# RWKV-7 recurrence on one core: the two heads of a pair on opposite partition halves, their matmuls alternating

## The chip, the cores and the metric

The kernel runs on 1 core of a Trainium2 chip. The metric is the device time of one execution in microseconds (us), taken as the median of several runs; less is better. TensorE (PE) does the matmuls, VectorE (DVE), ScalarE (ACT) and GpSimd (POOL) work on tiles, SyncE (SP) issues most transfers (DMA).

## What is computed

The program is a two-layer decoder trunk over 1024 tokens of 1024 channels. Layer 1 is an RWKV-7 time mix (16 heads of 64 channels) and an MLP, layer 2 is sliding-window attention and an MLP. The change lies in the state recurrence of layer 1, which the reference states as:

```python
def step(S, inp):
    r_t, w_t, k_t, v_t, a_t, b_t = inp
    sa = jnp.einsum('bhvk,bhk->bhv', S, a_t)
    S = S * w_t[:, :, None, :] + sa[..., None] * b_t[:, :, None, :] + v_t[..., None] * k_t[:, :, None, :]
    y = jnp.einsum('bhvk,bhk->bhv', S, r_t)
    return S, y
```

Per head, S is 64 x 64. Both kernels compute it in chunks of 64 tokens: within a chunk the dependence of tokens on each other is the inverse T of a triangular 64 x 64 matrix, so that a chunk takes a handful of 64 x 64 products per head.

## The kernel before

The large products (projections, MLP, output products) are float32 split into two 12-bit parts, three matmuls for each (mm3, L134 to L136), on tiles of 128 x 128 weights and 512 or 256 moving columns. The recurrence uses plain float32 matmuls; each of these stands in the trace as two matmul instructions ("rows" below), each with its own weight load.

The recurrence goes over 16 units: 8 blocks of 128 tokens (2 chunks each) times 2 groups of 8 heads (4 pairs). A unit passes through six steps, which the method recurrence calls in the order c i s p f j for most units: prep (p: the factors of the unit after the next), inner (i: inner products of the next unit's chunks, L638), solve (s: the 32 x 32 diagonal blocks of T by substitution, on GpSimd, in and out of DRAM), join (j: T's off-diagonal blocks, 32 x 32 matmuls L693 and L697), chunks (c: the chunks in turn), finish (f: norm, bonus and gate). In a chunk five batches of 8 matmuls (one per head) follow each other: L723 (the old state's and the values' part of u), L728 (their part of y), L733 (T times it, which gives u), L737 (the new state), L742 (u's part of y).

SV has the state (later u) of a head on partitions 0 to 63 and its values on 64 to 127, for all heads alike. So the matmuls of a batch of L723, L733 or L737 write the same 64 partitions of PSUM for all 8 heads; those of L728 and L742 write y by channels, where the odd head of a pair stands on the upper partitions, and so alternate between the two halves (h % 2).

A scheduler orders each engine's instructions from the code's order, priorities and its own estimate of times; the order is fixed when the program is built. The recurrence is emitted as urgent, which puts its instructions ahead of the large products where both are ready; the projections and, for units 8 to 15, the first MLP fill the rest. SP takes its transfers in this fixed order too, weight loads (L269, five tiles "wr") among those of the recurrence.

Of the kernel before, what the change touches and what calls it, by code (L numbers as in the profile page):

```python
# [50 lines left out]
# what follows what in a step of the recurrence: c chunks, i inner, s solve, p prep, j join, f finish;  # L51
# where the next block waits for its part, where the one after it does, elsewhere
# [22 lines left out]
class Trunk:  # L75
# [51 lines left out]
    def split(self, hi, lo, src, engine=None):  # L127
        """hi + lo = src; src is float32 in SBUF."""
# [10 lines left out]
    def consts(self):  # L139
# [19 lines left out]
        # derived columns: 1 - mu, w0 / 2, a0 / 2, k_a / 2, 1 - k_a / 2  # L159
# [6 lines left out]
        # masks of a chunk: rows s (twice), columns t (r side, a side)  # L166
# [7 lines left out]
        # head indicators  # L174
# [12 lines left out]
        # projection of a head's channels onto those of mean 0  # L187
# [6 lines left out]
        # reset of the running sum at each chunk  # L194
# [3 lines left out]
        # rows of the identity, dealt over partitions (js, block, chunk and head)  # L198
# [19 lines left out]
    def rsqrt(self, dst, src, mul, add):  # L218
        """dst = (src * mul + add) ** -0.5 for a narrow tile."""
# [25 lines left out]
    def turn_split(self, rows, gain):  # L245
        """Normalized rows by channels in two parts."""
# [18 lines left out]
    def weight(self, ap, shape, gain=None):  # L265
        """A weight of 2 KB a partition in two parts; gain: the columns of factors of its rows."""
# [11 lines left out]
    def prod_t(self, W, xs, c0, n=P):  # L278
        """[n outputs from c0 on, tokens] = (x W)^T in PSUM."""
# [7 lines left out]
    def prod_n(self, W, xs, j, n=512, gain=None):  # L287
        """Per token tile [P tokens, n] = columns j*n... of x W in PSUM; W has 128 rows for each of xs."""
# [10 lines left out]
    def mlp(self, layer, xt, rows, dst, G=4, between=None, beside=iter(()), pace=1):  # L299
        """xt: the rows, and what is added to them; rows: normalized; between: what is emitted before the last groups."""  # L300
# [35 lines left out]
    def steps(self, hT, n):  # L336
        """Differences of the tokens before and the tokens; none where there is no room for them."""
# [9 lines left out]
    def shifted(self, hT, i, n):  # L347
        """Per tile of channels, token-shifted input i in two parts."""
# [14 lines left out]
    def thin(self, hT, i, n, W, outs):  # L363
        """Input i times W, by tiles of channels; outs: (PSUM for [outputs, tokens], first column of W)."""
# [10 lines left out]
    def lora_out(self, W2, u, off, dst, pt):  # L375
        """tanh((u W2 + off) / 2) to DRAM, a channel tile at a time; u is float32 [64, tokens]."""
# [23 lines left out]
    def gate_in(self, hT, pt):  # L400
        """The gate's inner products, a channel tile at a time."""
# [18 lines left out]
    def gate_out(self, pt):  # L420
        """The gate to DRAM, a channel tile at a time."""
# [31 lines left out]
    def rows(self, pt):  # L453
        """Per 256 tokens, the normalized rows of a part; the first ones ahead."""
# [8 lines left out]
    def channels(self, pairs, hT):  # L463
        """Per 256 tokens, the normalized input by channels, with the token before; yields per two tiles of channels."""
# [17 lines left out]
    def project(self, pt, hT, left):  # L482
        """The projections of a part; left: what is left to do for the one before. Returns both for the next part."""
# [17 lines left out]
        # where there is room for both inputs, receptance and keys of a group before those of the next  # L501
# [15 lines left out]
        def prod(i, o):  # L517
            """Receptance, keys."""
# [8 lines left out]
        for group in groups:  # L527
# [3 lines left out]
            # and the squared norms of the keys' directions  # L531
# [24 lines left out]
            # 1 / max(|kk|, 1e-12)  # L556
# [6 lines left out]
    def spread(self, src, ps):  # L563
        """[P channels of a head pair, tokens] in PSUM = the values of the pair's heads, src: [P tokens, tiles, 2]."""
# [9 lines left out]
    def prep(self, blk, g):  # L574
        """Factors of the inner products of chunks; (head of a pair, channel of the head) is on partitions."""
# [8 lines left out]
        # running sums of the log decay and their exponentials  # L584
# [23 lines left out]
        nc.vector.tensor_tensor(bk[:, :, 0:L], v3(k), v3(a), ALU.mult)  # L608
        nc.vector.tensor_tensor(bk[:, :, L:], v3(m1), v3(w), ALU.mult)
# [485 lines left out]
```

## Time and profile before

| | us |
|---|---|
| median of 3 runs (2713.31 to 2717.18) | 2713.62 |
| span of the profiled execution | 2711.8 |
| PE busy, of its span | 2613.8 (96%) |
| DVE, ACT, POOL busy | 1678.5, 1297.1, 620.1 |

An engine's busy time is the union of its instructions' times, so overlapping matmuls count once. The span and the busy times are those of the profiled execution; the median is that of the timed runs.

### The profile page before, as it was taken

The page shows a single profiled execution, that of the slowest core. Times are in us where ns is not written, and L with a number is a line of the kernel's source. Part 1 is how long each engine was busy: PE and PEld are TensorE (multiplying, and loading weights), DVE is VectorE, ACT ScalarE, POOL GpSimd, SP SyncE. Part 2 cuts the span into 40 slices and gives each one's busy share as a digit, 9 for nine tenths or more (in the row PEclk, how much of TensorE's full clock was granted, in tenths as well). Part 3 has the DMA queues.
Part 4 walks back from the last instruction along what each step waited for, and adds up shares of the span by engine and source line. Part 5 has one row for each costly group of instructions (what it writes and reads, how often), then busy time and mean ns, then how long its engine had stood idle before and what let it go on. Part 6 is the DMA issues. An engine that isn't in the chain of part 4 may idle for free.

```text
span 2711.8 us, 43053 instructions
## 1 busy us (share of the span) xinstructions
PE 2613.8 (96%) x15226; PEld 2135.8 (79%) x15226; DVE 1678.5 (62%) x3252; ACT 1297.1 (48%) x2702; POOL 620.1 (23%) x1197
## 2 busy tenths in 40 slices
PE   6989989989989999999999999999999999999999
PEld 5867867766778788888788888888888888888887
DVE  8688688656666666644558777444899634444444
ACT  5565576445444333333365545434656533434342
POOL 6277634641454444330010000000000000000000
PEclk9989898989989999999999999999999999999999
DMA  5666544644634344333434434342445433433333
GB/s 176 197 185 168 162 114 122 170 114 147 181 88 115 104 111 112 96 95 94 159 94 137 147 118 141 105 159 82 139 140 195 128 98 93 124 94 100 94 99 97
DMA packets 428345, 345.43 MB, mean 127 GB/s; under 512 B 78672, under 2 KB 350176, under 8 KB 428128
## 3 DMA queue, kind: packets, MB, share of 16 engines
q1 hardware_dynamic: 411232, 340.57, 42.2%
q10 hardware_dynamic: 16896, 2.10, 0.5%
q8 instruction: 120, 1.97, 0.3%
q14 instruction: 97, 0.79, 0.1%
HBM read 276.51 MB, written 57.67 MB: 123 GB/s over the span
## 4 chain that ended last, share of the span: by engine, by line
PE 78%; POOL 8%; DVE 5%; DMA 5%; issue 2%; ACT 1%; SPq 1%; ACTq 0%; DVEq 0%; POOLq 0%
PE big L134 22%; PE big L135 22%; PE big L136 22%; POOL tmp L674 3%; POOL TT L676 3%; PE sm L638 2%; PE sq L723 1%; DMA Xs<-dXs 1%; PE sq L737 1%; PE sq L733 1%; DMA ld<-dP 1%; POOL m2k L130 1%; DVE wl L130 1%; DMA dXs<-XT 1%; PE sq L697 1%
## 5 line engine op out<-in xcount | busy, mean ns | idle before, releaser
L129 ACT CAST wh<-wr 128x512 fp32r<-128x512 f32 x741 | 458.5, 620 | 862.4 <-PE big L136 445.0
L130 DVE TENSOR_TENSOR wl<-wr,wh 128x512 fp32r<-128x512 f32 x741 | 522.7, 708 | 516.5 <-issue 227.9
L134 PE MATMUL big<-m2k,wh 128*128 128x512 f32 (+4 forms) x1528 | 577.6, 381 | 12.4 <-ACT m2k L129 5.6
L135 PE MATMUL big<-wl,m2k 128*128 128x512 f32 (+1 forms) x1472 | 574.9, 392 | 6.4 <-DVE wl L130 4.5
L135 PE MATMUL big<-m2k,wh 128*128 128x512 f32 (+4 forms) x1528 | 572.0, 375 | 7.7 <-DVE m2k L130 4.3
L136 PE MATMUL big<-m2k,wl 128*128 128x512 f32 (+3 forms) x1528 | 571.5, 376 | 3.2 <-DVE wl L130 3.2
L136 PE MATMUL big<-wh,m2k 128*128 128x512 f32 (+1 forms) x1472 | 562.1, 390 | 1.8 <-POOL m2k L130 1.5
L134 PE MATMUL big<-wh,m2k 128*128 128x512 f32 (+1 forms) x1472 | 513.7, 392 | 10.4 <-ACT m2k L129 6.7
L134 PEld LDWEIGHTS big<-m2k,wh 128*128 128x128 f32 (+2 forms) x1528 | 290.5, 191 | 75.2 <-ACT m2k L129 7.8
L135 PEld LDWEIGHTS big<-m2k,wh 128*128 128x128 f32 (+2 forms) x1528 | 290.6, 190 | 62.8 <-POOL m2k L130 6.1
L136 PEld LDWEIGHTS big<-m2k,wl 128*128 128x128 f32 (+2 forms) x1528 | 290.6, 190 | 56.6 <-DVE wl L130 4.8
L134 PEld LDWEIGHTS big<-wh,m2k 128*128 128x128 f32 x1472 | 278.8, 190 | 70.3 <-ACT m2k L129 8.0
L135 PEld LDWEIGHTS big<-wl,m2k 128*128 128x128 f32 x1472 | 280.0, 190 | 66.9 <-DVE wl L130 9.3
L136 PEld LDWEIGHTS big<-wh,m2k 128*128 128x128 f32 x1472 | 279.0, 190 | 59.0 <-POOL m2k L130 2.0
L674 POOL TENSOR_TENSOR tmp<-Xs,TT 128x60 f32<-128x60 f32 (+24 forms) x496 | 198.7, 401 | 142.4 <-DMA Xs<-dXs 105.7
L130 DVE TENSOR_TENSOR m2k<-relu,m2k 128x512 fp32r<-128x512 f32 (+1 forms) x200 | 132.8, 669 | 127.2 <-ACT m2k L129 126.8
L676 POOL TENSOR_TENSOR TT<-TT,tmp 128x60 f32<-128x60 f32 (+24 forms) x496 | 197.4, 398 | 37.8
L129 ACT CAST m2k<-relu 128x512 fp32r<-128x512 f32 (+1 forms) x272 | 146.4, 544 | 52.9 <-DVE relu L353 28.6
L322 DVE TENSOR_TENSOR b<-b,big 128x512 f32<-128x512 f32 x192 | 125.0, 680 | 17.5 <-PE big L136 17.0
L223 POOL TENSOR_TENSOR qn<-qn,mhalf 128x8 f32<-128x8 f32 x16 | 26.7, 1671 | 398.7 <-DVE qn L222 345.4
L223 POOL TENSOR_TENSOR ss<-ss,mhalf 128x4 f32<-128x4 f32 (+1 forms) x10 | 8.9, 888 | 475.2 <-DVE ss L222 475.1
L314 ACT ACTIVATE relu<-relu 128x512 f32<-128x512 f32 x128 | 80.8, 632 | 3.3
(231 smaller groups left out, 3250.9 us busy)
## 6 DMA issues: line engine op xcount, KB each, us to landing
wr<-in_mlp_w SPq DMA_DIRECT2D x512, 256.0 KB, 2.8
wr<-in_a_w_rkv SPq DMA_DIRECT2D x144, 256.0 KB, 3.9
ld<-dP SPq DMA_DIRECT2D x16, 1024.0 KB, 6.6
dS<-sc SPq DMA_DIRECT2D x28, 512.0 KB, 2.9
row<-dS SPq DMA_DIRECT2D x112, 128.0 KB, 3.0
dP<-stg SPq DMA_DIRECT2D x64, 128.0 KB, 2.7
AR<-RA SPq DMA_DIRECT2D x32, 256.0 KB, 4.6
Xs<-dXs SPq DMA_DIRECT2D x64, 128.0 KB, 3.0
```

Source lines behind the costliest of these rows:

```text
L129: self.nc.scalar.copy(hi, src)
L130: (engine or self.nc.vector).tensor_tensor(lo, src, hi.bitcast(F32), ALU.subtract)
L134: mm(ps, ah, bh, start=start, stop=False)
L135: mm(ps, ah, bl, start=False, stop=False)
L136: mm(ps, al, bh, start=False, stop=stop)
L223: nc.gpsimd.tensor_tensor(dst, dst, self.mhalf[:, :n], ALU.pow)
L314: nc.scalar.activation(r, r, AF.Square)
L322: nc.vector.tensor_tensor(v, v, ps[tt], ALU.add)
L638: nc.tensor.matmul(pg[:, ri, c], bk[hs, i], RA[hs, i], start=True, stop=True)
L674: nc.gpsimd.tensor_tensor(v, Xs[:, k:k + 1, k + 1:].broadcast_to([P, m, n]), TT[:, 0:m, k:k + 1].broadcast_to([P, m, n]), ALU.mult)
L676: nc.gpsimd.tensor_tensor(TT[:, 0:m, k + 1:], TT[:, 0:m, k + 1:], v, ALU.add)
L697: nc.tensor.matmul(ps[64:96, q * B:(q + 1) * B], XTq[96:128, q, 0:B], RTq[96:128, q, B:], start=True, stop=True)
```

## The change

Of each pair, the odd head now has everything on the opposite half. The method sides gives, for a head hp of a pair, its channels' half (hs), the half of the state, b~ and u (bs) and the half of k~ and the values (ks). In SV, the even head keeps the state below and the values above, the odd head has the values below and the state above; AR, BK, RT and XT follow. All batches go over the pairs with the even and the odd head in turn, so that neighbours write different halves of PSUM's partitions, and in L752, L766, L705 and L711 also read different halves. PSUM results of 8 heads by 64 rows become 4 pairs by 128 rows. The state lies by pairs on 128 partitions. The update is (S + product) times the decay instead of the two scaled and added, which takes the scaled copy in pb away. The values are loaded by four transfers instead of one, and once more for the bonus (L731); T's blocks go out and back in twice as many, smaller transfers. Core of the diff (the rest takes comments away):

```diff
@@ prep
-        EL = t("EL", [D, GP, 2, NC], 3)
-        for hp in range(2):
-            nc.vector.tensor_copy(EL[:, :, hp], ec[hp * D:(hp + 1) * D, :, L].rearrange("p (r c) -> p r c", c=NC))
+        EL = t("EL", [P, GP, NC], 3)
+        nc.vector.tensor_copy(EL, ec[:, :, L].rearrange("p (r c) -> p r c", c=NC))
...
-        nc.vector.tensor_tensor(bk[:, :, 0:L], v3(k), v3(a), ALU.mult)
-        nc.vector.tensor_tensor(bk[:, :, L:], v3(m1), v3(w), ALU.mult)
+        for hp in range(2):
+            hs, bs, ks = self.sides(hp)
+            nc.vector.tensor_tensor(bk[hs, :, bs], v3(k)[hs], v3(a)[hs], ALU.mult)
+            nc.vector.tensor_tensor(bk[hs, :, ks], v3(m1)[hs], v3(w)[hs], ALU.mult)
...
+    def sides(self, hp):
+        lo, up = slice(0, L), slice(L, P)
+        return (up, up, lo) if hp else (lo, lo, up)
@@ inner
+        for r0 in range(0, GP * NC, n):
+            pg = [self.small().rearrange("p (i m) -> p i m", i=n) for _ in range(2)]
+            for i in range(n):
+                for hp in range(2):
+                    hs = self.sides(hp)[0]
+                    nc.tensor.matmul(pg[hp][:, i], bk[hs, r0 + i], RA[hs, r0 + i], start=True, stop=True)
...
@@ solve
+        for hp in range(2):
+            r = self.sides(hp)[2].start
+            nc.gpsimd.memset(RT[r + B:r + L, hp, :, 0:B], 0.0)
+            for b in range(2):
+                nc.sync.dma_start(RT[r + b * B:r + (b + 1) * B, hp, :, b * B:(b + 1) * B],
+                                  dT[:, :, b, hp].rearrange("j s q i -> (j s) q i"))
@@ join
+        for q in range(n):
+            for hp, b, k in sides:
+                nc.tensor.matmul(ps[k + B:k + L, q], XT[b:b + B, q, B:], XT[b:b + B, q, 0:B], start=True, stop=True)
...
+        for q in range(n):
+            for hp, b, k in sides:
+                nc.tensor.matmul(ps[k:k + B, q], AT[k + B:k + L, q], RT[k + B:k + L, hp, q, B:], start=True, stop=True)
@@ chunks
+        heads = [(pi, *x) for pi in range(GP) for x in sides]
...
+            for c in range(NC):
+                nc.sync.dma_start(SV[ks, c, hp], dV[c * L:(c + 1) * L].rearrange("l (r h d) -> l h r d", h=2, d=D)[:, hp])
...
+        nc.sync.dma_start(bv[L:].rearrange("l c h d -> l c (h d)"), dV.rearrange("(c l) d -> l c d", l=L))
...
-            for h in range(GH):
-                nc.tensor.matmul(ps[L:, h], AR[:, h // 2, h % 2, c, L:], SV[:, c, h], start=True, stop=True)
+            for pi, hp, bs, ks in heads:
+                nc.tensor.matmul(ps[ks, pi], AR[:, hp, pi * NC + c, L:], SV[:, c, hp, pi], start=True, stop=True)
...
-            nc.vector.tensor_tensor(pb[0:D], SV[0:D, c], el, ALU.mult)
...
-            for h in range(GH):
-                nc.tensor.matmul(ps[0:L, h], RT[L:, h, c], pb[L:, h], start=True, stop=True)
-            nc.vector.tensor_copy(SV[0:L, c], ps[0:L])
+            for pi, hp, bs, ks in heads:
+                nc.tensor.matmul(ps[bs, pi], RT[ks, hp, pi * NC + c], pb[ks, pi], start=True, stop=True)
+            for hp, bs, ks in sides:
+                nc.vector.tensor_copy(SV[bs, c, hp], ps[bs])
...
-            nc.vector.tensor_tensor(nxt, ps[0:D], el, ALU.mult)
-            nc.vector.tensor_tensor(nxt, nxt, pb[0:D], ALU.add)
+            nc.vector.tensor_tensor(sn, ps, S, ALU.add)
+            if c < NC - 1:
+                for hp, bs, ks in sides:
+                    nc.vector.tensor_tensor(SV[bs, c + 1, hp], sn[bs], el[bs], ALU.mult)
+            nc.vector.tensor_tensor(S, sn, el, ALU.mult)
...
-                nc.tensor.matmul(py[h % 2 * D:(h % 2 + 1) * D, h // 2], SV[0:L, c, h], RT[0:L, h, c], start=True, stop=True)
+                nc.tensor.matmul(py[bs, pi], SV[bs, c, hp, pi], RT[bs, hp, pi * NC + c], start=True, stop=True)
```

The order that the scheduler makes of it, at two places. On PE, the inner products of unit 8 (RA, bk: its factors; tiles sm are PSUM banks, before one for two pairs of one head side; now the first of two belongs to the even heads): before,

```order
L134 MATMUL big_8769<-wh_8826,m2k_8734 128x512
L135 MATMUL big_8769<-wl_8827,m2k_8734 128x512
L136 MATMUL big_8769<-wh_8826,m2k_8735 128x512
L638 MATMUL sm_8486<-RA_8150,bk_8151 128x128 x4
L638 MATMUL sm_8497<-RA_8150,bk_8151 128x128 x4
L134 MATMUL big_8766<-wh_8844,m2k_8740 128x512
L135 MATMUL big_8766<-wl_8845,m2k_8740 128x512
L134 MATMUL big_8767<-wh_8844,m2k_8740 128x512
L135 MATMUL big_8767<-wl_8845,m2k_8740 128x512
```

and now

```order
L134 MATMUL big_8824<-wh_8845,m2k_8777 128x512
L135 MATMUL big_8824<-wl_8846,m2k_8777 128x512
L642 MATMUL sm_8520<-RA_8189,bk_8190 128x128
L642 MATMUL sm_8521<-RA_8189,bk_8190 128x128
L642 MATMUL sm_8520<-RA_8189,bk_8190 128x128
L642 MATMUL sm_8521<-RA_8189,bk_8190 128x128
L642 MATMUL sm_8520<-RA_8189,bk_8190 128x128
L642 MATMUL sm_8521<-RA_8189,bk_8190 128x128
L642 MATMUL sm_8520<-RA_8189,bk_8190 128x128
L642 MATMUL sm_8521<-RA_8189,bk_8190 128x128
L136 MATMUL big_8821<-wh_8845,m2k_8778 128x512
L136 MATMUL big_8822<-wh_8845,m2k_8778 128x512
```

The second half of the same step stands now as

```order
L136 MATMUL big_8823<-wh_8881,m2k_8790 128x512
L134 MATMUL big_8824<-wh_8881,m2k_8789 128x512
L642 MATMUL sm_8536<-RA_8189,bk_8190 128x128 x4
L642 MATMUL sm_8537<-RA_8189,bk_8190 128x128 x4
L135 MATMUL big_8824<-wl_8882,m2k_8789 128x512
L136 MATMUL big_8824<-wh_8881,m2k_8790 128x512
L134 MATMUL big_8821<-wh_8899,m2k_8795 128x512
```

Before, each x4 is one bank's four (pair, chunk) products of one head side; now both sides' products alternate in the first piece and stand in two blocks of four in the second. Over the whole program there are 8 fully alternating runs of eight, 9 of the second kind, 8 in which two or three products stand in a row before the sides change, and 14 blocks of four with other work between. The batches of eight of the chunks and of the join alternate throughout; their rows read alike before and now, since the names do not tell the halves.

On SP, the loads of values (SV, and now bv) of unit 10 among the weight loads (wr) of the first MLP: before,

```order
L269 DMA wr_12656<-in_mlp_w 128x512
L269 DMA wr_12674<-in_mlp_w 128x512
L708 DMA SV_9905<-dV_169 64x2x512
L269 DMA wr_12692<-in_mlp_w 128x512
L269 DMA wr_12718<-in_mlp_w 128x512
L269 DMA wr_12736<-in_mlp_w 128x512
L654 DMA Xs_10067<-dXs_10068 32x1024 x4
L269 DMA wr_12754<-in_mlp_w 128x512
L269 DMA wr_12772<-in_mlp_w 128x512
L778 DMA dZ_171<-z_9829 128x4x128
```

and now

```order
L269 DMA wr_12615<-in_mlp_w 128x4x128
L269 DMA wr_12633<-in_mlp_w 128x4x128
L728 DMA SV_9974<-dV_169 64x4x64 x4
L269 DMA wr_12659<-in_mlp_w 128x4x128
L269 DMA wr_12677<-in_mlp_w 128x4x128
L269 DMA wr_12703<-in_mlp_w 128x4x128
L661 DMA Xs_10133<-dXs_10134 32x1024 x4
L269 DMA wr_12721<-in_mlp_w 128x4x128
L269 DMA wr_12750<-in_mlp_w 128x512
L269 DMA wr_12768<-in_mlp_w 128x512
L269 DMA wr_12786<-in_mlp_w 128x512
L731 DMA bv_9981<-dV_169 64x2x512
```

One transfer became four, and the load of bv, which waits for PE's transposes of the unit before, stands among weight loads.

## Rows read from the trace of the kernel before

**Rows 1.** The page's head and part 1: busy us (share of span), instructions.

```profile
span 2711.8 us, 43053 instructions
...
PE 2613.8 (96%) x15226; PEld 2135.8 (79%) x15226; DVE 1678.5 (62%) x3252; ACT 1297.1 (48%) x2702; POOL 620.1 (23%) x1197
```

**Rows 2.** Windows by stage: from:to, length, busy of engines, clock, DMA share, GB/s.

```profile
190.00:770.00 580.00, 535.27 (x4090) 424.16 (x4089) 402.71 (x832) 312.06 (x685) 280.23 (x562) 0.92 0.52 146
770.00:1290.00 520.00, 515.80 (x3777) 421.38 (x3776) 305.82 (x577) 207.34 (x405) 192.26 (x449) 0.97 0.37 102
1290.00:2710.00 1420.00, 1410.39 (x6492) 1168.06 (x6490) 828.64 (x1578) 667.75 (x1356) 42.51 (x35) 1.00 0.39 121
```

**Rows 3.** PE by line and shape: shapes, count, busy us, mean ns, idle before.

```profile
L638 PE MATMUL sm<-RA,bk 64*128 64x128 f32 x512 | 75.5, 294 | 0.0
...
L723 PE MATMUL sq<-SV,AR 128*64 128x64 f32 x512 | 39.0, 233 | 1.1 <-DVE SV L739 1.1
L737 PE MATMUL sq<-SV,BK 128*64 128x64 f32 x512 | 37.4, 228 | 0.1
L733 PE MATMUL sq<-pb,RT 64*64 64x64 f32 x512 | 37.3, 224 | 0.0
...
L728 PE MATMUL sq<-AR,SV 128*64 128x64 f32 x512 | 26.8, 238 | 0.0
...
L742 PE MATMUL sq<-RT,SV 64*64 64x64 f32 x512 | 22.2, 227 | 0.0
L693 PE MATMUL sq<-XT 32*32 32x32 f32 x512 | 20.5, 197 | 9.6 <-DVE XT L690 9.6
L697 PE MATMUL sq<-RT,XT 32*32 32x32 f32 x512 | 19.8, 194 | 0.1
```

**Rows 4.** PE in order of time, two stretches: start, length, instructions merged.

```profile
459.85 1.16 PE L638 MATMUL sm<-RA,bk 64*128 64x128 f32 x8
460.93 0.50 PE L135 MATMUL big<-wl,m2k 128*128 128x512 f32 x1
...
463.42 0.69 PE L728 MATMUL sq<-AR,SV 128*64 128x64 f32 x16
464.04 1.14 PE L733 MATMUL sq<-pb,RT 64*64 64x64 f32 x16
465.11 0.50 PE L134 MATMUL big<-m2k,wh 128*128 128x512 f32 x1
...
473.01 1.15 PE L737 MATMUL sq<-SV,BK 128*64 128x64 f32 x16
474.08 0.68 PE L742 MATMUL sq<-RT,SV 64*64 64x64 f32 x16
474.70 0.55 PE L658 MATMUL sm<-ident,bk 128*128 128x128 f32 x3
...
966.48 1.19 PE L697 MATMUL sq<-RT,XT 32*32 32x32 f32 x32
967.61 1.15 PE L723 MATMUL sq<-SV,AR 128*64 128x64 f32 x16
```

**Rows 5.** What PE waited for: us in total, times, longest.

```profile
PE sq L693 <- DVE XT L690: 9.6, 3, 7.1
```

**Rows 6.** Windows before and in a half-clock stretch (columns as rows 2).

```profile
965.00:969.80 4.80, 4.80 (x72) 4.15 (x70) 2.71 (x6) 1.78 (x3) 4.09 (x10) 1.00 0.54 159
969.80:976.70 6.90, 6.90 (x33) 5.18 (x32) 1.81 (x4) 0.88 (x2) 5.63 (x17) 0.51 0.65 192
```

**Rows 7.** SP's longest wait, and the bonus product's wait on POOL (min/median/max ns).

```profile
SPq L269 <- DVE wl L130: 1305.3, 563, 12.5
...
L712 POOLq EVENT_SEMAPHORE  x17: 17/7336/20029, 97.2 to 1216.0; - x17
```

**Rows 8.** DVE by line and shape (columns as rows 3).

```profile
L729 DVE TENSOR_TENSOR pb<-SV,EL 64x512 f32<-64x512 f32 x32 | 23.0, 718 | 0.2
...
L608 DVE TENSOR_TENSOR bk<-ld 128x512 f32<-128x512 f32 x16 | 11.9, 744 | 0.0
```

More of the change, by code (lines that the diff above doesn't have):

```diff
@@ L649, in inner @@
+        for hp in range(2):
+            hs = self.sides(hp)[0]
+            nc.sync.dma_start(AR[hs, hp], RA[hs])
         Xs = t("Xs", [P, B, B])
-        dX = self.dp.tile([2, NQ, B, B], F32, tag="dXs", name=self.nm("dXs"), bufs=2)
+        dX = self.dp.tile([2, 2, NQ // 2, B, B], F32, tag="dXs", name=self.nm("dXs"), bufs=2)
         for b in range(2):
-            nc.scalar.dma_start(dX[b].rearrange("q k i -> k q i"), XTq[b * B:(b + 1) * B, :, b * B:(b + 1) * B])
+            for hp in range(2):
+                r = hp * L + b * B
+                nc.scalar.dma_start(dX[b, hp].rearrange("q k i -> k q i"), XT[r:r + B, :, b * B:(b + 1) * B])
@@ L666, in solve @@
         AR, BK, RT, EL, bonus, XT, Xs = made
-        XTq, RTq = (x.rearrange("p h c l -> p (h c) l") for x in (XT, RT))
         TT = t("TT", [P, B // JS, B])
@@ L676, in solve @@
             nc.gpsimd.tensor_tensor(TT[:, 0:m, k + 1:], TT[:, 0:m, k + 1:], v, ALU.add)
[L677 to L682 removed]
+        dT = self.dp.tile([B // JS, JS, 2, 2, NQ // 2, B], F32, tag="dTT", name=self.nm("dTT"), bufs=2)
+        nc.sync.dma_start(dT.rearrange("j s b h q i -> (s b h q) j i"), TT)
+        for hp in range(2):
+            r = self.sides(hp)[2].start
[3 more added lines that the diff above has]
+                                  dT[:, :, b, hp].rearrange("j s q i -> (j s) q i"))
         return made
@@ L688, in join @@
         AR, BK, RT, EL, bonus, XT, Xs = made
-        XTq, RTq = (x.rearrange("p h c l -> p (h c) l") for x in (XT, RT))
-        nc.vector.transpose(XTq[0:B, :, 0:B], RTq[L:L + B, :, 0:B])
-        ps = self.turn()
-        for q in range(NQ):
-            nc.tensor.matmul(ps[96:128, q * B:(q + 1) * B], XTq[0:B, q, B:], XTq[0:B, q, 0:B], start=True, stop=True)
-        nc.scalar.copy(XTq[96:128, :, 0:B], ps[96:128].rearrange("p (q i) -> p q i", i=B))
-        ps = self.turn()
-        for q in range(NQ):
-            nc.tensor.matmul(ps[64:96, q * B:(q + 1) * B], XTq[96:128, q, 0:B], RTq[96:128, q, B:], start=True, stop=True)
-        nc.scalar.copy(RTq[64:96, :, B:], ps[64:96].rearrange("p (q i) -> p q i", i=B))
+        n = NQ // 2
+        sides = [(hp, self.sides(hp)[1].start, self.sides(hp)[2].start) for hp in range(2)]
+        for hp, b, k in sides:
+            nc.vector.transpose(XT[b:b + B, :, 0:B], RT[k:k + B, hp, :, 0:B])
+        AT = self.t(self.rp, "AT", [P, n, B], F32)
+        ps = self.turn().rearrange("p (q i) -> p q i", i=B)
+        for q in range(n):
+            for hp, b, k in sides:
+                nc.tensor.matmul(ps[k + B:k + L, q], XT[b:b + B, q, B:], XT[b:b + B, q, 0:B], start=True, stop=True)
+        for hp, b, k in sides:
+            nc.scalar.copy(AT[k + B:k + L], ps[k + B:k + L, 0:n])
+        ps = self.turn().rearrange("p (q i) -> p q i", i=B)
+        for q in range(n):
+            for hp, b, k in sides:
+                nc.tensor.matmul(ps[k:k + B, q], AT[k + B:k + L, q], RT[k + B:k + L, hp, q, B:], start=True, stop=True)
+        for hp, b, k in sides:
+            nc.scalar.copy(RT[k:k + B, hp, :, B:], ps[k:k + B, 0:n])
         return AR, BK, RT, EL, bonus
@@ L706, in chunks @@
         AR, BK, RT, EL, bonus = made
-        SV = t("SV", [P, NC, GH, D])
-        nc.sync.dma_start(SV[L:].rearrange("l c h d -> l c (h d)"),
-                          self.dV[pt][t0:t0 + TB, g * GH * D:(g + 1) * GH * D].rearrange("(c l) d -> l c d", l=L))
-        nc.vector.tensor_copy(SV[0:D, 0], self.state[g])
+        SV = t("SV", [P, NC, 2, GP, D])
+        sides = [(hp, *self.sides(hp)[1:]) for hp in range(2)]
+        heads = [(pi, *x) for pi in range(GP) for x in sides]
+        dV = self.dV[pt][t0:t0 + TB, g * GH * D:(g + 1) * GH * D]
@@ L713, in chunks @@
+        nc.gpsimd.tensor_tensor(bv[L:], bv[L:], bonus[L:].unsqueeze(3).broadcast_to([L, NC, GH, D]), ALU.mult)
         y = t("y", [P, GP, NC, L])
         def bank():
-            return self.turn().rearrange("p (h d) -> p h d", d=D)
+            return self.turn().rearrange("p (h d) -> p h d", d=D)[:, 0:GP]
+        S = self.state[g]
         for c in range(NC):
-            nxt = SV[0:D, c + 1] if c < NC - 1 else self.state[g]
-            el = EL[:, :, :, c].rearrange("p r h -> p (r h)").unsqueeze(2).broadcast_to([D, GH, D])
+            el = EL[:, :, c].unsqueeze(2).broadcast_to([P, GP, D])
@@ L721, in chunks @@
             ps = bank()
-            for h in range(GH):
-                nc.tensor.matmul(ps[L:, h], AR[:, h // 2, h % 2, c, L:], SV[:, c, h], start=True, stop=True)
-            pb = t("pb", [P, GH, D])
-            nc.scalar.copy(pb[L:], ps[L:])
+            for pi, hp, bs, ks in heads:
+                nc.tensor.matmul(ps[ks, pi], AR[:, hp, pi * NC + c, L:], SV[:, c, hp, pi], start=True, stop=True)
+            pb = t("pb", [P, GP, D])
+            nc.scalar.copy(pb, ps)
             py = bank()
-            for h in range(GH):
-                nc.tensor.matmul(py[h % 2 * D:(h % 2 + 1) * D, h // 2], SV[:, c, h], AR[:, h // 2, h % 2, c, 0:L], start=True, stop=True)
@@ L729, in chunks @@
-            nc.vector.tensor_tensor(pb[0:D], SV[0:D, c], el, ALU.mult)
-            nc.scalar.copy(y[:, :, c], py[:, 0:GP])
+            for pi, hp, bs, ks in heads:
+                nc.tensor.matmul(py[bs, pi], SV[:, c, hp, pi], AR[:, hp, pi * NC + c, 0:L], start=True, stop=True)
+            nc.scalar.copy(y[:, :, c], py)
             ps = bank()
-            for h in range(GH):
-                nc.tensor.matmul(ps[0:L, h], RT[L:, h, c], pb[L:, h], start=True, stop=True)
-            nc.vector.tensor_copy(SV[0:L, c], ps[0:L])
+            for pi, hp, bs, ks in heads:
+                nc.tensor.matmul(ps[bs, pi], RT[ks, hp, pi * NC + c], pb[ks, pi], start=True, stop=True)
@@ L735, in chunks @@
+            for hp, bs, ks in sides:
+                nc.vector.tensor_copy(SV[bs, c, hp], ps[bs])
             ps = bank()
-            for h in range(GH):
-                nc.tensor.matmul(ps[0:D, h], BK[:, h // 2, c, h % 2], SV[:, c, h], start=True, stop=True)
-            nc.vector.tensor_tensor(nxt, ps[0:D], el, ALU.mult)
-            nc.vector.tensor_tensor(nxt, nxt, pb[0:D], ALU.add)
+            for pi, hp, bs, ks in heads:
+                nc.tensor.matmul(ps[bs, pi], BK[:, pi * NC + c, hp], SV[:, c, hp, pi], start=True, stop=True)
@@ L1023, in trunk @@
     with tc.tile_pool(name="rwkv", bufs=1) as k.rp:
-        states = k.rp.tile([P, GH, D], F32, name="states")
+        states = k.rp.tile([P, NG, GP, D], F32, name="states")
         tc.nc.vector.memset(states, 0.0)
-        k.state = [states[g * D:(g + 1) * D] for g in range(NG)]
+        k.state = [states[:, g] for g in range(NG)]
         hT, left = [], iter(())
```

50 lines of the change are left out of this document (18 added, 32 removed).

## The prediction

> **What bounds the kernel.** I read busy times first. PE is busy for 2613.8 of 2711.8 us [rows 1], so at most 98 us of the span are anything but PE. Next the windows by stage [rows 2]: the recurrence lies between 190 and 1290 us; PE is idle there for 580.0 - 535.3 = 44.7 us before 770 us and 4.2 us after it, and from 1290 us on the change touches nothing. A cut in PE's own work shortens the run almost one to one, and the latency of the recurrence's chain counts only where PE waits for it. Then PE's time by line [rows 3]: the eight lines that the change turns cost 75.5 + 39.0 + 37.4 + 37.3 + 26.8 + 22.2 + 20.5 + 19.8 = 278.5 us, a tenth of the run.
>
> What a batch costs is read from the order of time [rows 4], from one batch's start to the next one's, since lengths overlap. The reader is to compare batches of the same eight products, 16 rows each. L733, all in one place of the array, takes 465.11 - 464.04 = 1.07 us; L737, also in one place, 474.08 - 473.01 = 1.07 us. L728 and L742, which write the two halves of PSUM's partitions in turn, take 464.04 - 463.42 = 0.62 and 474.70 - 474.08 = 0.62 us. L728 has the same 128 x 64 shape as L737, L742 the 64 x 64 of L733. So the kernel before already shows the effect of alternation: two matmuls on different halves of columns run beside each other, and a batch costs 0.45 us less. Busy times agree: 37.3 against 22.2 us over 512 / 16 = 32 batches is 0.47 us a batch [rows 3].
>
> **The change part by part.** The sum is made against the profiled execution: 2711.8 us of span and 1.8 us around it are the median, 2713.6.
>
> First, L723, L733 and L737 alternate. 3 lines x 32 batches x 0.45 us = 43.2 us. The ends: with busy times, L733 to L742 on all three lines gives 3 x 15.1 = 45.3; L723 and L737 to L728's 26.8 gives 12.2 + 10.6 + 15.1 = 37.9 [rows 3]. I take 43. L728 and L742 alternate before and now: 0, while the new pairs of L742 overlap as the old ones do (a rival below).
>
> Second, the join's 32 x 32 products, 2 lines x 16 batches of 32 rows. A batch takes 967.61 - 966.48 = 1.13 us, 35 ns a row; L742's alternating rows go at 0.62 / 16 = 39 ns each, the entry to another shape included [rows 4]. No row of the trace goes clearly faster than the join's already do, so the gain may be nothing; if two run beside each other, half of 20.5 + 19.8 is saved, 20 us [rows 3]. I take 6, nearer to the lower end, since the nearest row speaks for it.
>
> The Trainium skill, "TensorE: Matmul & The Clock Gate", section "Wait — 56ns, not 53.3ns?", says that matmuls never start less than about 25 ns apart however small they are. The rows above stay over it, so nothing contradicts it; by it the join would gain at most an estimated 1024 x (35 - 25) = 10 us, and the sum below would be 66 instead of 62.
>
> Third, the inner products, L638 to L642. They would alternate between the halves of the rows of the array, into two banks; no row of before shows that. One product (two rows) takes 1.08 / 4 = 0.27 us (459.85 to 460.93, four products [rows 4]). The order shows that not all alternate: 8 runs of eight do and would save 8 x 4 x 0.27 = 8.6 us; 9 runs of four and four overlap only where the side changes, 9 x 0.27 = 2.4; in 8 mixed ones two products overlap, 8 x 0.54 = 4.3; blocks apart save nothing. Together 15.3 at most and 0 at least. With the share that column halves reached (0.45 of the 0.535 that halving 1.07 would give) it is 13, which I take, because the column halves are the nearest rows.
>
> So PE loses 43 + 6 + 13 = 62 us of work.
>
> What other engines get. DVE: the scaled copy L729 goes, 23.0 us; the two products for bk become four of half the partitions and the same columns, about twice 11.9 us more [rows 8]; the masks and copies trade fewer, longer instructions for more, shorter ones. The net is near nothing, and DVE is busy for 306 of the 520 us of the later stage [rows 2], so a few us are covered there; before 770 us, at 403 of 580, less so. SP: per unit the values' load becomes four, one for bv is new, T's return becomes four instead of two, six transfers more. SP spends 1305 us waiting for weight tiles to come free [rows 7], so it has room as long as none of the new ones blocks (a rival below). GpSimd's solve is untouched.
>
> Waits of PE. Before 770 us, where half of the 16 units lie, half of the saving (31 us) falls among waits of 44.7 us. Of those the join's wait for T is 9.6 us in three places [rows 5], at the end of a chain of GpSimd and transfers that doesn't get shorter. Where PE comes earlier to such a wait, the gain since the last one is lost. The bounds are 0 and 31; I take 8, a quarter, because most chains there begin with PE's own work and move along with it, and because PE waits for next to nothing in the later stage.
>
> The clock. In 969.8 to 976.7 us the granted clock is 0.51, so nearly all of it at the 1.2 GHz level, after 4.8 us in which PE was never idle but ran 72 rows, mostly small ones [rows 6]. Over the stage 0.92 and 0.97 were granted [rows 2], which is 0.08 x 580 + 0.03 x 520 = 62 us lost. Shorter runs of small matmuls should bring fewer such stretches, but a half-busy array may bring others. I take 4 us of gain, between 10 of loss and 12 of gain.
>
> Sum: 62 - 8 + 4 = 58 us; 2713.6 - 58 = 2656.
>
> **The rivals.** One: different rows and one bank. In L752 (T's product), L766 and the join, neighbours differ in the half that they read as well as in the half that they write, but both write one PSUM bank. If two halves of rows can't write a bank at once, L733 gains nothing, L742 loses the overlap that it has (32 x 0.45 = 14.4), the join gains nothing; L723 and L737 keep 28.8, the inner products, in two banks, 13. That is 27 us, less 4 for waits: 2691. For it: no row of before reads two halves in turn. Against it: L728 and L742 write two halves of one bank at full overlap [rows 4].
>
> The Trainium skill, "TensorEngine Tiling (Array Packing)", section "Gotcha 1: PSUM Pressure", says just this, that different row tiles cannot access the same PSUM bank simultaneously. No run here shows it; by it the 2691 of this rival would be the time.
>
> Two: everything overlaps and nothing waits: 43 + 20 + 13 + 4 = 80 us, 2634. For it: PE waits only 4.2 us after 770 us.
>
> Three: neither the join nor the inner products gain (no row shows them alternating) and waits take 16: 43 - 16 = 27, 2687.
>
> Four, slower: the load of bv stands in SP's queue among weight loads and must wait until PE has transposed the bonus tile of the unit before; behind it stand the weights that PE needs next. Before, only GpSimd waited at that place: 7.3 us in the median, 20.0 at most [rows 7]. The five weight tiles cover it: in the last stage a matmul takes 1420 / 6492 = 0.219 us [rows 2], a tile feeds 12 of them (three for each of four token tiles), so five last 13 us. From a wait of 13 us on PE stalls; at 5 us over, in each of 16 units, 80 us are lost: 2713.6 - 58 + 80 = 2736. Against it: the scheduler puts the load near the time at which it expects the tile to be free.
>
> Five, no change: the recurrence's chain sets the pace and PE waits where it worked: 2713. Against it: the 4.2 us. That the change doesn't do what it says holds for the inner products in part, and is priced above.
>
> **How the numbers follow.** The likeliest, 2656: 0.55. Everything overlaps, 2634: 0.14. One bank, 2691: 0.14. Join and inner products without gain, 2687: 0.08. No change: 0.03. Weights held up: 0.06. The range from 2634 to 2694 leaves out half of the second case, part of the third, and the last two, about 0.18 in all. Faster by over 0.2% (5.4 us, about what a measurement of this kernel can tell from no change) are the first four, 0.91; within it 0.03; slower 0.06.
>
> **What would show it.** In the changed kernel PE's busy time should stand near 2613.8 - 62 = 2552 us and its idle time near 106. L743, L752 and L757 should be busy for 22 to 27 us each, L766 still about 22; if L752 is near 37 and L766 too, the one-bank rival holds. The join's two lines should have 17 us each rather than 10 or 20, L642 about 62. The granted clock of 190 to 770 us should be a little over 0.92. A row of PE waiting for weights, with SP's bv load before it, would show the fourth. I am wrong if PE's busy time falls by the sum and the span doesn't, or if alternating rows turn out to run one after the other.

## The result, and the profile after

The changed kernel takes 2683.82 us in the median of 4 runs (2681.72 to 2687.1) against 2713.47 for the one before: the ratio is 0.9889, 95% interval 0.9875 to 0.9903. That is 30 us faster where 58 were forecast. The time lies within the range and above the predicted 2656.

The page of the changed kernel, span and busy us:

```profile
span 2682.1 us, 43180 instructions
...
PE 2549.6 (95%) x15226; PEld 2066.2 (77%) x15226; DVE 1688.0 (63%) x3204; ACT 1289.1 (48%) x2670; POOL 616.9 (23%) x1213
```

Beside [rows 1], PE's busy time fell by 2613.8 - 2549.6 = 64.2 us, but the span by 29.7 only. PE's idle time rose from 98.0 to 2682.1 - 2549.6 = 132.5 us. So the work went and half of the room became waiting. The windows by stage tell where (columns as in [rows 2]):

```profile
190.00:770.00 580.00, 514.15 (x4249) 397.57 (x4249) 416.43 (x827) 314.35 (x684) 285.20 (x601) 0.92 0.53 153
770.00:1290.00 520.00, 501.88 (x3773) 400.74 (x3772) 321.85 (x584) 213.30 (x410) 190.66 (x430) 0.98 0.41 117
1290.00:2680.00 1390.00, 1381.66 (x6369) 1145.82 (x6367) 810.25 (x1547) 654.88 (x1334) 39.71 (x31) 1.00 0.38 119
```

Idle time before 770 us is now 580.0 - 514.15 = 65.9 us, 21 more than in [rows 2]; from 770 to 1290 us it is 18.1, 14 more. The granted clock is as it was, 0.92 and 0.98. PE's lines, to be held against [rows 3]:

```profile
L642 PE MATMUL sm<-RA,bk 64*128 64x128 f32 x512 | 56.5, 293 | 6.7 <-DVE RT L648 4.8 <-ACT wh L129 1.8
L743 PE MATMUL sq<-SV,AR 128*64 128x64 f32 x512 | 27.5, 240 | 13.2 <-issue 12.8
L748 PE MATMUL sq<-AR,SV 128*64 128x64 f32 x512 | 26.3, 241 | 1.2 <-ACT RT L713 1.0
L757 PE MATMUL sq<-SV,BK 128*64 128x64 f32 x512 | 25.6, 232 | 4.4 <-DVE SV L754 4.3
L752 PE MATMUL sq<-pb,RT 64*64 64x64 f32 x512 | 22.7, 230 | 2.0 <-ACT pb L745 2.0
L766 PE MATMUL sq<-RT,SV 64*64 64x64 f32 x512 | 22.3, 227 | 0.0
L705 PE MATMUL sq<-XT 32*32 32x32 f32 x512 | 12.2, 195 | 8.9 <-DVE XT L700 8.9
L711 PE MATMUL sq<-RT,AT 32*32 32x32 f32 x512 | 12.0, 193 | 0.3
```

The mean length of one instruction is as before (227 to 241 ns in the chunks, 224 to 238 in [rows 3]), the busy time of a line is not: the matmuls got no shorter, they overlap. The eight lines together went from 278.5 to 205.1 us. The last column has what is new: 13.2 us of idle time ahead of L743, the first batch of a chunk, where [rows 3] had 1.1 ahead of L723. Batches in order of time, columns as in [rows 4]:

```profile
463.44 0.68 PE L752 MATMUL sq<-pb,RT 64*64 64x64 f32 x16
464.06 0.66 PE L570 MATMUL sm<-ident,wide 128*128 128x128 f32 x4
...
469.30 0.69 PE L757 MATMUL sq<-SV,BK 128*64 128x64 f32 x16
469.91 0.68 PE L766 MATMUL sq<-RT,SV 64*64 64x64 f32 x16
```

A batch of T's product takes 464.06 - 463.44 = 0.62 us and one of the new state 0.61; both took 1.07 in [rows 4]. That is the 0.45 us on which the sum was built.

**The new wait.** From 770 to 1290 us the waits of PE have one row that matters (line waited for: us in total, times, longest):

```profile
PE sq L743 <- issue: 12.8, 6, 3.2
```

"Issue" means that the profile names no releaser, so the reader must look at the engine that makes L743's input. That is the state, written into SV for the second chunk by DVE's L762. DVE's own waits, now and (second fence, from the kernel before) then:

```profile
DVE XT L700 <- DMA RT<-dTT: 80.1, 17, 8.2
```

```profile
DVE XT L690 <- DMA RT<-dTT: 51.5, 13, 8.4
```

The join's transposes of T wait for T's transfer out of DRAM. That cost PE little before; the order of time, all engines, shows why it costs now (start, length, what; in brackets the idle time ahead):

```profile
1018.41 0.42 DVE L759 TENSOR_TENSOR sn<-sq,states 128x256 f32<-128x256 f32 x1
...
1024.25 1.82 SPq L689 DMA_DIRECT2D RT<-dTT  x4
...
1026.34 0.43 DVE L700 STREAM_TRANSPOSE XT<-RT 32x256 f32<-32x256 f32 x1 [7.51 <-DMA RT<-dTT]
1026.80 0.87 DVE L762 TENSOR_TENSOR SV<-sn,EL 64x256 f32<-64x256 f32 x2
...
1027.32 1.42 PE L743 MATMUL sq<-SV,AR 128*64 128x64 f32 x15 [3.19 <-issue]
```

DVE has the new state sn ready at 1018.8 (1018.41 + 0.42). The next instruction in its fixed order is not the state's scaling into SV (L762), but the next unit's transpose L700, whose data are issued by SP only at 1024.25. DVE stands for 7.51 us, L762 comes behind it, and PE, which had filled the time with the large products that it had, stops for 3.19 us before L743. The first L700 stands ahead of the state's scaling in six units in a row, 9 to 14: in five of them behind L759 (here unit 12 in the built program, the one of the rows above), in unit 14 ahead even of L759:

```
L759 TENSOR_TENSOR sn_10856<-sq_10847,states 128x256
L700 STREAM_TRANSPOSE XT_10928<-RT_10927 32x8x32
L762 TENSOR_TENSOR SV_10804<-sn_10856,EL_10266 64x256 x2
```

In the kernel before, L690 is the fourth or fifth instruction behind the state's L739 in these units, so that its wait comes after the state has been written; here unit 11, all of DVE's rows:

```profile
984.79 0.68 DVE L739 TENSOR_TENSOR SV<-SV,pb 64x512 f32<-64x512 f32 x1
985.51 0.68 DVE L729 TENSOR_TENSOR pb<-SV,EL 64x512 f32<-64x512 f32 x1
986.85 0.69 DVE L130 TENSOR_TENSOR wl<-wr,wh 128x512 fp32r<-128x512 f32 x1 [0.66 <-PE big L136]
988.53 0.69 DVE L130 TENSOR_TENSOR wl<-wr,wh 128x512 fp32r<-128x512 f32 x1 [0.99 <-PE big L135]
991.58 0.70 DVE L690 STREAM_TRANSPOSE XT<-RT 32x512 f32<-32x512 f32 x1 [2.35 <-DMA RT<-dTT]
```

The pause costs more than itself; windows ahead of it, in it and behind it (columns as in [rows 2]):

```profile
1017.00:1024.00 7.00, 6.98 (x53) 5.23 (x53) 1.80 (x3) 4.03 (x7) 3.99 (x13) 1.00 0.16 28
1024.00:1027.30 3.30, 0.13 (x1) 0.01 (x1) 0.90 (x3) 0.00 (x0) 0.40 (x1) 0.97 0.52 100
1027.30:1034.00 6.70, 6.68 (x49) 5.52 (x49) 6.56 (x13) 1.37 (x3) 0.00 (x0) 0.76 0.40 116
```

The granted clock is 1.00 before, and 0.76 over the 6.7 us after the engine stood: about half of that stretch at the lower of the two levels, 1.2 instead of 2.4 GHz (an estimate, (1.00 - 0.76) / 0.5).

### The profile page after: what moved, and what is told of

Same layout as the page of the kernel before. It is cut to its first block, busy times and chain, and to the rows that moved or that the text cites. A ratio compares the mean times of both kernels' runs of the same rounds, so it can differ in the third digit from the quotient of the medians.

```text
span 2682.1 us, 43180 instructions
## 1 busy us (share of the span) xinstructions
PE 2549.6 (95%) x15226; PEld 2066.2 (77%) x15226; DVE 1688.0 (63%) x3204; ACT 1289.1 (48%) x2670; POOL 616.9 (23%) x1213
## 4 chain that ended last, share of the span: by engine, by line
PE 54%; DVE 2%; DMA 0%; ACT 0%; issue 0%; POOL 0%; DVEq 0%; ACTq 0%; POOLq 0%
PE big L134 17%; PE big L135 17%; PE big L136 17%; PE sm L134 1%; PE sm L135 0%; PE sm L136 0%; PE sq L956 0%; PE sq L957 0%; PE big L252 0%; DVE sc L962 0%; DVE wl L130 0%; DVE m2k L260 0%; PE sq L933 0%; DMA wr<-in_b_wq 0%; DVE b L1038 0%; DVE st L966 0%
## 5 line engine op out<-in xcount | busy, mean ns | idle before, releaser
L130 DVE TENSOR_TENSOR wl<-wr,wh 128x512 fp32r<-128x512 f32 x741 | 529.4, 718 | 485.5 <-issue 226.0
L134 PE MATMUL big<-m2k,wh 128*128 128x512 f32 (+3 forms) x1528 | 576.4, 380 | 9.8 <-ACT m2k L129 4.8
L136 PE MATMUL big<-m2k,wl 128*128 128x512 f32 (+2 forms) x1528 | 571.3, 376 | 7.4 <-DVE wl L130 7.3
L135 PE MATMUL big<-m2k,wh 128*128 128x512 f32 (+2 forms) x1528 | 571.1, 375 | 7.3 <-POOL m2k L130 4.2
L134 PEld LDWEIGHTS big<-m2k,wh 128*128 128x128 f32 (+1 forms) x1528 | 290.3, 190 | 70.8 <-ACT m2k L129 6.9
L136 PEld LDWEIGHTS big<-m2k,wl 128*128 128x128 f32 (+1 forms) x1528 | 290.8, 191 | 59.6 <-DVE wl L130 10.1
L135 PEld LDWEIGHTS big<-m2k,wh 128*128 128x128 f32 (+1 forms) x1528 | 290.6, 190 | 58.5 <-POOL m2k L130 6.7
L135 PEld LDWEIGHTS big<-wl,m2k 128*128 128x128 f32 x1472 | 282.1, 192 | 69.2 <-DVE wl L130 10.4
```

The source lines that it names most:

```text
L130: (engine or self.nc.vector).tensor_tensor(lo, src, hi.bitcast(F32), ALU.subtract)
L134: mm(ps, ah, bh, start=start, stop=False)
L135: mm(ps, ah, bl, start=False, stop=False)
L136: mm(ps, al, bh, start=False, stop=stop)
```

## The experiments

Lines behind an inserted piece have other numbers: L746 to L769 in e1 are L743 to L766 of the changed kernel. All ratios are to the kernel before on the same chip. Two profiles of one kernel (e1 and its repetition) differ by 8 us in the idle time before 770 us (65.2 and 57.0), so the conclusions below rest on the ratios.

**Is it the place of the transposes?** e1 ties the join's transposes to the end of the unit's chunks: a copy of one element of y (the transpose writes over it afterwards) comes ahead of them.

```diff
-    def join(self, made):
+    def join(self, made, y=None):
...
+        if y is not None:
+            for hp, b, k in sides:
+                nc.vector.tensor_copy(XT[b:b + B, 0, 0:1], y[b:b + B, 0, NC - 1, L - 1:L])
...
-                            made = self.join(nxt)
+                            made = self.join(nxt, y)
```

> The changed kernel, with the transposes at the head of the join (two on VectorE) kept behind the last y of the chunks before by a one-column copy that they overwrite. Theory A (VectorE's fixed order): in the changed kernel TensorE's idle time rose from 98 to 132 us mainly because these transposes stand ahead of the state's update and wait up to 8 us for T's transfer, with the update and the next batch L743 behind them. Then the idle time falls by 15 to 20 us, L743's own 13 us go, and the time is 2662 to 2670. Theory B (TensorE only uncovers waits that stood there already, since its own work got shorter): the idle time stays near 130 us and the time near 2684.

Measured: 2655.91 us, ratio 0.9768 (0.9749 to 0.9787). The two stages of e1:

```profile
190.00:770.00 580.00, 514.81 (x4294) 397.04 (x4292) 421.80 (x850) 318.51 (x690) 285.00 (x593) 0.93 0.54 154
770.00:1290.00 520.00, 517.30 (x3867) 413.30 (x3864) 332.27 (x612) 217.12 (x420) 196.94 (x438) 1.00 0.44 124
```

Idle time from 770 to 1290 us is 2.7 us instead of 18.1, and the clock is 1.00 there. DVE's wait is down from 80.1 us:

```profile
DVE XT L703 <- DMA RT<-dTT: 30.7, 7, 8.7
```

Ahead of L746, the first batch of a chunk, PE's idle time is 0.6 us instead of 13.2. So theory A holds and theory B falls, with a time below theory A's range. The time fell by 0.0121 x 2713 = 33 us (26 to 39 by the two intervals, an estimate), more than the 15.4 us of idle time taken out of this stage. The clock of the stage, 1.00 instead of 0.98, is worth another 0.02 x 520 = 10 us, and PE's whole busy time fell from 2549.6 to 2531.8 us (2539.7 when e1 ran again, 2544.5 in e1b). Slower stretches like that after 1027.3 fit this; what they cost was not measured apart.

e1b ties the transposes to the last chunk's values in SV instead, so that they may come before y is complete:

```diff
-                nc.vector.tensor_copy(XT[b:b + B, 0, 0:1], y[b:b + B, 0, NC - 1, L - 1:L])
+                nc.vector.tensor_copy(XT[b:b + B, 0, 0:1], y[b:b + B, NC - 1, hp, 0, 0:1])
...
-                            made = self.join(nxt, y)
+                            made = self.join(nxt, self.SV)
```

> As the run before, but the transposes are only kept behind the update of the state for the second chunk, so that they may still stand within that chunk. Theory A: the wait of the second chunk's L743 goes, and T has mostly landed by then; 2664 to 2676. Theory B: 2684.

Measured: 2656.55 us, ratio 0.9764 (0.9746 to 0.9782), idle from 770 to 1290 us 4.1 us. Its range too was missed on the low side. It is enough that the transposes come after the state for the second chunk; how far after makes no difference that the intervals could tell.

**What does alternation alone do?** e2 has the changed kernel's layout and transfers, but each batch goes through one side and then the other, so that the side changes once in a batch; inner and join likewise.

```diff
-        heads = [(pi, *x) for pi in range(GP) for x in sides]
+        heads = [(pi, *x) for x in sides for pi in range(GP)]
```

> The changed kernel with all its layout, but in every batch first the four even heads, then the four odd ones, so that sides change once instead of seven times. The price of alternation alone: of the 160 batches of the chunks each loses about three quarters to seven eighths of 0.45 us (54 to 63 us), the join about 14, the inner products 15: TensorE busy 2630 to 2645 us. Theory A: the order on VectorE is another one and decides the idle time, which may fall to 100 to 120. Theory B: the idle time returns to 98 with the work. Time by both 2735 to 2760; by the idle time they differ.

Measured: 2693.73 us, ratio 0.9906 (0.9888 to 0.9924): faster than the kernel before, with one change of side in a batch. The forecast of 2735 to 2760 missed: PE is busy for 2593.7 us instead of 2630 to 2645, and idle for 2697.8 - 2593.7 = 104.1, as theory A had it. PE's lines of e2:

```profile
L766 PE MATMUL sq<-RT,SV 64*64 64x64 f32 x512 | 31.4, 227 | 0.0
L752 PE MATMUL sq<-pb,RT 64*64 64x64 f32 x512 | 31.0, 224 | 0.2 <-ACT pb L745 0.2
```

and one of its batches, with what follows on PE:

```profile
1007.92 0.96 PE L752 MATMUL sq<-pb,RT 64*64 64x64 f32 x16
1008.82 1.09 PE L617 MATMUL sm<-rk,ld 128*64 128x2 f32 x16
```

A batch with one change of side takes 0.90 us, against 1.07 with none [rows 4] and 0.62 with a change at each product. One change saves 0.17 of the 0.45 us. L766 rose from 22.3 to 31.4, so it is alternation that makes the overlap.

e2b joins the two, e2's order of sides and e1's place of the transposes.

> The run before with the join's transposes behind the chunks. Against the first run of this job it is alternation alone at one order on VectorE. Theory A: idle time as in the first run within 8 us, so the difference in time is the difference in TensorE's busy time, 80 to 95 us. Theory B: alternation uncovers waits here too, and a third to a half of the difference in busy time is lost.

Measured: 2682.78 us, ratio 0.9864 (0.9848 to 0.9879). Alternation is worth 0.9864 - 0.9768 = 0.0096, some 26 us, with the transposes late (e2b to e1), but only 0.0017, some 5 us and within the intervals, with the transposes where the scheduler had put them (e2 to the changed kernel). That is not the same place in both: in e2's trace only two of units 9 to 14 have L700 ahead of L762 (1086.90 and 1152.40 us), so this pair compares two orders on DVE as well. Of the 2584.6 - 2531.8 = 52.8 us of busy time between e2b and e1, 120.3 - 96.6 = 23.7 came back as idle time, nearly half, as e2b's theory B had it. The idle time before 770 us is 42.8 us in e2b and 41.5 in e2, near the 44.7 of before, against 65.2 and 65.9 where the sides alternate. So it is alternation, not the layout or its additional transfers, that brings the additional waits there, 22 to 24 us in these two pairs.

**Where is alternation worth something?** e3 and e4, on e1's basis, alternate in half of the units (inner and join have the same condition):

```diff
+        u = blk * 2 + g
-        heads = [(pi, *x) for pi in range(GP) for x in sides]
+        heads = [(pi, *x) for pi in range(GP) for x in sides] if u < 8 else [(pi, *x) for x in sides for pi in range(GP)]
```

e4 has u >= 8 in that place. e1 and e2b ran again with them on the same chip.

> On the basis of e1 (transposes of the join behind the chunks). The two heads of a pair alternate only in units 0 to 7, which lie mostly before 770 us; in units 8 to 15 the sides go one after the other. Theory, early saving lost: before 770 us PE's work falls by about 22 us against e2b but its idle time rises by about as much (from 43 to 60 or more), so the whole time stays within 6 us of e2b: ratio 0.983 to 0.987. Rival, saving worth the same everywhere: half of the 26 us between e2b and e1 is gained here, ratio about 0.982 or less.

> On the basis of e1, alternation only in units 8 to 15. Theory, early saving lost: idle time before 770 us falls back to about 43 us, after 770 us it stays at 2 to 4 us, and the whole time stays within 6 us of e1: ratio 0.976 to 0.979. Rival, saving worth the same everywhere: half of the difference between e2b and e1 is missing, ratio about 0.981 or more.

> e1 again, on the chip of e3 and e4, as the end with alternation in all units: ratio 0.975 to 0.979.

> e2b again, on the chip of e3 and e4, as the end with alternation in no unit: ratio 0.985 to 0.988.

| alternation in | us | ratio to before, 95% | PE busy, us | idle before 770 us |
|---|---|---|---|---|
| no unit (e2b again) | 2677.64 | 0.9857 (0.9839 to 0.9875) | 2584.3 | 39.4 |
| units 0 to 7 (e3) | 2680.10 | 0.9865 (0.9845 to 0.9884) | 2569.1 | 61.0 |
| units 8 to 15 (e4) | 2655.26 | 0.9773 (0.9753 to 0.9793) | 2549.0 | 46.9 |
| all units (e1 again) | 2652.99 | 0.9766 (0.9747 to 0.9786) | 2539.7 | 57.0 |

The stage before 770 us in e2b again, e3, e4 and e1 again, one fence each:

```profile
190.00:770.00 580.00, 540.65 (x4308) 430.31 (x4307) 423.83 (x849) 316.83 (x689) 293.13 (x616) 0.94 0.54 154
```

```profile
190.00:770.00 580.00, 518.99 (x4244) 401.43 (x4242) 417.32 (x839) 316.17 (x687) 282.80 (x593) 0.92 0.53 153
```

```profile
190.00:770.00 580.00, 533.10 (x4319) 423.75 (x4317) 427.21 (x853) 319.81 (x695) 296.37 (x621) 0.95 0.54 154
```

```profile
190.00:770.00 580.00, 523.05 (x4327) 404.91 (x4325) 426.14 (x854) 321.62 (x696) 286.36 (x601) 0.92 0.53 154
```

All four ratios lie where they were expected, and the rival that the saving is worth the same everywhere falls. Alternation in the first eight units takes 15 us of busy time from PE and puts 22 us of idle time in their place; alternation in the last eight takes 35 and gives back 10. With it, e3 and e1 again pass the early stage at a granted clock of 0.92, without it, e2b again and e4 at 0.94 and 0.95. That would be 0.02 to 0.03 x 580 = 12 to 17 us, contained in the busy time, and may be why only 15 us came off there; it is an estimate from one profile each. Over all timed runs the clock of the whole span, 0.977 against 0.980 (e3, e2b again) and 0.976 against 0.981 (e1 again, e4), makes it 6 to 12 us.

**Which part of the early alternation is lost?** A first guess was the inner products: with both sides in turn, two PSUM banks (tiles sm) fill side by side, and PE then waits until DVE's masks have read them; in e3, 11.2 us of PE's idle time ahead of writes to sm before 770 us end with such a mask, in e2b again 1.3. e5 lets in the first eight units only chunks and join alternate, e6 only the inner products; the last eight alternate throughout.

> On the basis of e1. Only the inner products of the first eight units go one side after the other; chunks and join alternate in all units. Theory, banks of the inner products: where both sides' banks fill side by side, the next matmuls into a bank (sm) wait for DVE's masks; without it, PE's waits before 770 us for tiles sm that the masks release fall from 7 to 11 us to under 5, PE's idle time there from 57 to 65 us to 48 to 52 us, and the whole time is that of e1 or up to 6 us below it: ratio 0.974 to 0.977. Rival, the early stage fills any saving with waits wherever it comes from: idle time stays in proportion to the work saved, about 52 to 57 us, with waits elsewhere, and the ratio stays at 0.9765 to 0.978.

> On the basis of e1. In the first eight units only the inner products alternate, chunks and join go one side after the other. Theory, banks of the inner products: PE's waits for tiles sm that the masks release stand at 7 us or more, idle time before 770 us at 54 us or more, and the time is above that of e5: ratio 0.978 to 0.981. Rival, any saving is filled: idle time 50 to 53 us, ratio 0.977 to 0.978.

Measured: e5 2656.39 us, ratio 0.9772 (0.9757 to 0.9787); e6 2647.52 us, ratio 0.9744 (0.9729 to 0.9759), against 2717.25 for the kernel before. Their early stages, e5 and then e6:

```profile
190.00:770.00 580.00, 524.07 (x4264) 404.21 (x4262) 420.44 (x846) 316.75 (x687) 281.10 (x589) 0.92 0.54 153
```

```profile
190.00:770.00 580.00, 534.65 (x4325) 426.22 (x4324) 429.63 (x852) 320.19 (x692) 295.05 (x618) 0.94 0.54 153
```

The guess falls: the idle time and the lower clock go with the chunks and the join (e5: 55.9 us, 0.92), not with the inner products (e6: 45.3 us, 0.94), and the masks' waits were 6.6 and 5.9 us in the two. e5 came out as its rival said; e6 lies below the ranges of both its theory and its rival. e5 and e4 differ in that chunks and join alternate early in e5 alone, and their ratios are 0.9772 and 0.9773. e6 has the lowest time of all kernels run, though its interval overlaps those of e1, e4 and e5.

## Why the prediction came out as it did

**The work: right in sum.** PE lost 64.2 us of busy time where 62 were summed. That the two agree to 2 us is luck in part, since the errors of the terms cancel. The terms, by the rows after and [rows 3]: the chunks 11.5 + 14.6 + 11.8 = 37.9 us instead of 43, the lower of the two bounds; the join 40.3 - 24.2 = 16.1 instead of 6, since two small products do run beside each other; the inner products 75.5 - 56.5 = 19.0 instead of 13, over the bound of 15.3. That bound let only one product overlap where a block of four of one side follows one of the other; e2, in which no products alternate, already has 65.1 us on that line instead of 75.5, and that is 10.4 us for its 32 changes of side, where 32 x 0.27 = 8.6 would be the most by that count. The eight lines lost 278.5 - 205.1 = 73.4 us, and other lines, which the sum had at nothing, took 9 of it back.

**The waits: the step that failed.** They were taken as 8 us, with 31 as the bound, and measured at 132.5 - 98.0 = 34.5. The span then fell by 64.2 - 34.5 = 29.7 us. The prediction's own sign of being wrong, busy time that falls by the sum while the span does not, came true by half; that the time still lies in the range is owed to the range's upper end, drawn for other rivals. Two parts of the waits are told apart by the runs.

The first, 14 us of idle time between 770 and 1290 us, rests on the sentence that "PE waits for next to nothing in the later stage". That is true of the kernel before and says nothing of the order of the one after. L690's wait for T's transfer, 51.5 us on DVE, was there all along and harmless; moved one place ahead of the state's scaling, the same wait stops the recurrence. The order of DVE's instructions could be read before the run, and the prediction looked at PE's and SP's only. e1 and e1b show it: with that one dependence the time falls by 33 us more, to 0.9768 of the time before, 63 us less than before. That this is near the 58 forecast is chance, since the early loss stays in it.

The second, 21 us before 770 us, is of the kind that the prediction named, but it took a quarter of the early saving as lost, where the runs show lost all that alternation adds over a single change of side (e3 against e2b again: 0.9865 and 0.9857). "Most chains there begin with PE's own work and move along with it" was the reason given; e3 to e6 contradict it for chunks and join. The traces show where the saving ends. Unit 8 is the first whose tokens belong to the last projected part (512 to 1023), and its factors need the norms of that part's keys, which GpSimd computes in L560. The last state of unit 7 and L560 in e2b again and in e3:

```profile
662.73 0.43 DVE L766 TENSOR_TENSOR states<-sn,EL 128x256 f32<-128x256 f32 x1
...
664.55 10.55 POOL L560 TENSOR_TENSOR ssk<-ssk,mhalf 128x64 f32<-128x64 f32 x1 [30.00 <-DVE ssk L559]
```

```profile
652.18 0.42 DVE L773 TENSOR_TENSOR states<-sn,EL 128x256 f32<-128x256 f32 x1
...
668.00 10.55 POOL L560 TENSOR_TENSOR ssk<-ssk,mhalf 128x64 f32<-128x64 f32 x1 [0.83 <-DVE ssk L559]
```

With alternation the recurrence of the first eight units ends 662.73 - 652.18 = 10.6 us earlier, but the projections for which unit 8 waits end no earlier (PE's L570, the next step, stands 3.64 and 3.96 us until they come); e1 again and e4 show the same (649.79 and 661.73, L560 at 665.61 and 663.56). Why PE's freed time doesn't bring the projections forward is open. PE's additional waits are spread over masks, transposes and split weights, with no row over 10 us, and whether the lower clock follows from the pauses or from the half-used array was not separated.

**The clock.** 4 us of gain were taken; over the span it went from 0.973 to 0.974, an estimated 0.001 x 2682 = 2.7 us, and less than the changed kernel's own runs differ by (0.972 to 0.974). The stage after 770 us would have given more (1.00 in e1); with the pauses before L743 it stands at 0.98.

**The rivals.** One bank falls: L752 and L766 read and write different halves in turn, into one bank, and take 22.7 and 22.3 us, as L742 did in [rows 3]. The Trainium skill, "TensorEngine Tiling (Array Packing)", section "Gotcha 1: PSUM Pressure", says that different row tiles cannot access one bank at the same time; the trace shows no cost of it, and the 2691 of that rival didn't come. In these batches the two halves write different partitions of the bank; no run here has them write the same ones. SP's load of bv held nothing up; its lines in the trace (duration ns min/median/max, first and last start):

```profile
L731 SPq DMA_DIRECT2D bv<-dV x16: 585/588/3130, 52.4 to 1188.0; - x16
L731 SPq EVENT_SEMAPHORE  x13: 17/17/28, 265.1 to 1186.9; - x13
```

Its waits are 17 ns in the median and 28 at most, against the 13 us from which it would have decided. That everything overlaps was nearly so for the eight lines (73.4 us of that rival's 43 + 20 + 13 = 76), but not for the waits. The third rival's 2687 is close to the result for the wrong reason: join and inner products gained 35 us, and the loss came from elsewhere.

## What to carry to other kernels

When work is taken from the engine that bounds, price the order as well as the work: read in the built program what stands ahead of each step of the critical chain on the engines beside it, since a wait that was harmless behind that step stops everything when it stands in front. A dependence of one element, which ties a step that waits for a transfer to the end of the urgent work, is a cheap way to keep it behind. And count a saving only in those stages in which the engine is busy almost throughout; here, in a stage with 8% of idle time, none of the early saving was left that alternation in chunks and join adds; other work, the projections, ended that stage.

## What was not expected of the hardware

The join's 32 x 32 products, in order of time in the changed kernel:

```profile
808.07 0.69 PE L711 MATMUL sq<-RT,AT 32*32 32x32 f32 x32
808.69 0.69 PE L743 MATMUL sq<-SV,AR 128*64 128x64 f32 x16
```

32 rows take 808.69 - 808.07 = 0.62 us, 19 ns each on average, against 35 in [rows 4]. So rows on different halves start more closely than any did before; a pair, one row on each half, takes 39 ns. The Trainium skill, "TensorE: Matmul & The Clock Gate", section "Wait — 56ns, not 53.3ns?", has matmuls start no less than about 25 ns apart; over alternating halves the trace doesn't agree. A floor of that size on each half would not be contradicted by it.

That a single change of side in a batch of eight already saves 0.17 us (e2) was not expected either (an eighth to a quarter of 0.45 was), nor that among the kernels of the new layout the early stage's granted clock goes with the alternation of the chunks there: 0.91 to 0.93 in the six profiles with it (the changed kernel, e1, its repetition, e1b, e3, e5), 0.94 or 0.95 in the five without (e2, e2b, its repetition, e4, e6). The kernel before, which has neither, stands at 0.92 [rows 2], so the cause isn't known.
